# Moving SBUF tiles by 64 to 192 bytes: the start offsets of a PE-bound encoder layer's matmul operands

## The chip, the core and the metric

The kernel runs on one core of a Trainium2 chip. The metric is the device time of one execution in microseconds (us); three runs of the kernel before gave a median of 1275.18 us. One further execution was taken with the hardware profiler; views of its trace are quoted below.

## What is computed

One layer of a bidirectional encoder on 512 tokens of 1024 features, in float32: a half-step SwiGLU feed-forward block, a mixer (a dilated-window attention branch A, a grouped-query attention branch B, gates, an output projection), a second half-step SwiGLU, a final norm.

```python
x = x + 0.5 * swiglu(rmsnorm(x, g1), w1, w3, w2)       # 1024 -> 2816 -> 1024
h = rmsnorm(x, gm)
proj = h @ w_in                                        # A: q, k, v; B: q, k, v; gates
mix = (sigmoid(gA) * (o_a @ P_A) + sigmoid(gB) * (o_b @ P_B)) @ w_out
x = x + mix
x = x + 0.5 * swiglu(rmsnorm(x, g2), w1, w3, w2)
y = rmsnorm(x, g)
```

## The kernel before

**Products in three matmuls.** Every float32 operand is split into a high and a low part (a copy that rounds, then a subtraction), and each product is made of three matmuls on TensorE (PE) in `mm3`: high by high (L233), then the two mixed ones (L234 and L235). Each matmul has a stationary operand of 128 columns, loaded by its own weight load (PEld in the profile), and a moving operand of 256 or 512 columns that is streamed through. In the trace the load for a matmul begins as the matmul ahead of it begins: while one matmul's moving operand is read from SBUF, the stationary operand of the next is read from SBUF too.

**Weights.** All weights come in chunks of 128x1024 by DMA into raw tiles (`wr`, `wa`, `wt`, `ws`), are split by ScalarE (L218) and VectorE (L219) into a pair `wh`, `wl`, and one pair feeds 24 matmuls: 8 slices of 128 columns by three. Below, such a group of 24 is called a tile of work. There are three pairs in the pool `wb` (the main pairs). A fourth pair (tag `whx` in `prep`, L207) lies in whichever pool `self.wx` names, and serves each fourth chunk (`n % 4 == 3`) of the kinds `sw` and `w2`, and of `wb` while branch B's projection runs. In the trace all of them have the name `wh` or `wl`.

**Stages.** Each feed-forward block begins with plain products of 512 columns (`feat`, moving `hH`, `hL`). Then it alternates between stages of a Strassen-like scheme (`strassen`: moving operands of 256 columns from `hH`, `hL`, `TH`, `TL`; outputs `mm`, `X`, `Y`) and the down projection (`blocks`: moving `gg`, 512 columns). The first block has three such rounds, starting with 14, 28 and 21 tiles of 256-column work; the second has 21, 28 and 21. In the last round of the second block half of the down projection is done in 256 columns. The mixer first projects tokens (`token`: there the weights move, 512 columns, and `hH` is stationary), then has one stage of 35 tiles of 256-column work for q and k of branch A (moving `hH`, `TQH`), then 512-column work of many kinds between the attention steps, then `wab` and `wo` (moving `oH`, `qH`, `mH`). In all, 168 tiles of work have 256-column moving operands in these stages: 168 x 24 = 4032 matmuls. 41 of the 168 use the fourth pair.

**Where tiles lie.** Pools are stacked in SBUF from the left in the order in which they are opened, some from the right (`side="right"`: `hH`, `hL`, `TH`, `TL`, `V0`, `V1`). A tile's start byte (the same in each partition) is the sum of all that stands ahead of it. In the pool `tmp` the kernel before reserves a tile `even` of 64 bytes that nothing uses; all that is opened behind it from the left starts 64 bytes later for it. The order of the PE's instructions is written out by the program itself; the other engines' order is set by the recording layer.

Of the kernel before, what the change touches and what calls it, by code (L numbers as in the profile page):

```python
# [11 lines left out]
F32 = mybir.dt.float32  # L12
# [57 lines left out]
class Layer:  # L70
    def __init__(self, ctx, tc, a):
        self.tc, self.nc, self.a = tc, tc.nc, a
        ctx.enter_context(tc.manual_schedule(engines={mybir.EngineType.PE}))
        pool = lambda n, **k: ctx.enter_context(tc.tile_pool(name=n, **k))
        self.dram = pool("dram", bufs=1, space=DRAM)
        self.cst = pool("cst", bufs=1)
        self.wb = pool("wb", bufs=1)
        self.tmp = pool("tmp", bufs=4)
        self.tmp.tile([128, 16], F32, tag="even", name="even", bufs=1)
        self.psm = pool("psm", bufs=4, space=PSUM)  # L80
        self.psa = pool("psa", bufs=4, space=PSUM)
        nc = self.nc
        c = self.cst
        self.x = [c.tile([128, T], F32, name=f"x{d}") for d in range(NK)]
        self.par = c.tile([128, 48], F32, name="par")
        nc.scalar.dma_start(self.par, a["par"])
        self.ident = c.tile([128, 128], F32, name="ident")
        self.ones = c.tile([128, 1], F32, name="ones")
        nc.vector.memset(self.ones, 1.0)
        self.mhalf = c.tile([128, 4], F32, name="mhalf")  # L90
        nc.vector.memset(self.mhalf, -0.5)
        nc.scalar.activation(self.ones, self.ones, AF.Copy)
        self.r = c.tile([128, 8], F32, name="r")
        self.R = c.tile([128, T], F32, name="R")
        nc.gpsimd.memset(self.R, 0.0)
        self.acc = c.tile([128, T], F32, name="acc")
        self.open_h()
        self.gate_d = self.dram.tile([16, 128, T], F32, name="gate_d")
        self.qk_d = self.dram.tile([2 * NSQ, 128, T], F32, name="qk_d")
        self.items = ([("v", 0), ("v", 1), ("sw", 0), ("v", 2)] + [("g", j) for j in range(2)]  # L100
                      + [("qk", f) for f in range(NSQ, 12)] + [("g", j) for j in range(2, 9)]
                      + [("b", g) for g in range(3)] + [("g", j) for j in range(9, 16)])
        span = {"v": ("wav", 4), "qk": ("waq", 2), "g": ("wg", 1), "b": ("wb", 4)}
        self.order = self.ffn_order("a")
        for kind, n in self.items:
            if kind == "sw":
                self.order += [("swq", at) for at in self.slots(range(0, NSQ, 2))]
                continue
            name, m = span[kind]
            self.order += [(name, m * n + i) for i in range(m)]  # L110
        self.order += [("wab", i) for i in range(12)] + [("wo", i) for i in range(8)]
        self.order += self.ffn_order("b")
        self.raws, self.tiles, self.used, self.wx, self.TQ = {}, [], 0, None, None
        self.cap = len(self.order)
        self.rings = {k: [] for k in BUFS}
        self.index = {it[:2]: n for n, it in enumerate(self.order)}
        self.kind = [self.home(it) for it in self.order]
        self.todo = sorted((n for n, t in enumerate(self.kind) if t != "ws"), key=self.turn_of)
# [22 lines left out]
    def open_h(self):  # L141
        self.hctx = ExitStack()
        hp = self.hctx.enter_context(self.tc.tile_pool(name="hp", bufs=1, side="right", reuse_waits="tile"))
        self.hH = [hp.tile([128, T], F32R, name=f"hH{d}") for d in range(NK)]
        self.hL = [hp.tile([128, T], F32R, name=f"hL{d}") for d in range(NK)]

    def split(self, dst_pool, src, shape, tagH, tagL):
        nc = self.nc
# [265 lines left out]
    def ffn(self, s, gin, gnext, hooks, out=None, side=None):  # L414
        with ExitStack() as ctx:
            pool = lambda n, **k: ctx.enter_context(self.tc.tile_pool(name=n, reuse_waits="tile", **k))
            tp = pool("hT", bufs=1, side="right")
            self.TH = tp.tile([128, 3, 4, 256], F32R, name="TH")
            self.TL = tp.tile([128, 3, 4, 256], F32R, name="TL")
            self.wx = pool("wx", bufs=1)  # L420
            self.cp = pool("c", bufs=2)
            self.ffn_run(s, gin, gnext, hooks, out, side or {}, pool("g", bufs=1))
            self.wx = None

# [256 lines left out]
    def project_qk(self):  # L681
        nc, tc = self.nc, self.tc
        with ExitStack() as ctx:
            pool = lambda n, **k: ctx.enter_context(tc.tile_pool(name=n, reuse_waits="tile", **k))
            tp = pool("qT", bufs=1)
            self.TQ = [tp.tile([128, 4, 4, 256], F32R, name=f"TQ{c}") for c in "HL"]
            self.wx = pool("wxq", bufs=1)
            cp, qp = pool("cq", bufs=2), pool("qo", bufs=2)
            steps = self.tq_steps(cp)
            hooks = {7: self.stat_r, 12: self.stat_R, 17: self.stat_p}  # L690
            for n, _ in enumerate(self.stream(self.items[:2])):
                if n in hooks:
                    hooks[n]()
                if n > 8 and n % 4 == 0 and steps:
                    steps.pop(0)()
            assert not steps
            c = {}

            def scaled(dst, src, a, perm, neg):
                src, dst = src.rearrange("p (j n) -> p j n", j=2), dst.rearrange("p (j n) -> p j n", j=2)  # L700
                R = (self.acc if perm else self.R).unsqueeze(1).to_broadcast([128, 2, T])
                if perm:
                    src = src.rearrange("p j (m r) -> p j r m", r=4)
                    dst, R = (t.rearrange("p j (r m) -> p j r m", r=4)[:, :, :, 64 * a:64 * a + 64] for t in (dst, R))
                else:
                    dst, R = (t[:, :, 256 * a:256 * a + 256] for t in (dst, R))
                if neg:
                    for j in range(2) if perm else (slice(0, 2),):
                        nc.vector.scalar_tensor_tensor(dst[:, j], src[:, j], -1.0, R[:, j], op0=ALU.mult, op1=ALU.mult)
                else:  # L710
                    nc.vector.tensor_mul(dst, src, R)

            def store(f, part, t):
                i = 2 * f + part
                nc.gpsimd.dma_start(self.qk_d[i:i + 3:2].rearrange("c p n -> p c n"), t.rearrange("p (c n) -> p c n", c=2))

            def evict(f, step, ps):
                perm = PAIRS[f][1] > 0
                if step == "A11":
                    c[f] = (cp.tile([128, 1024], F32, tag="c1", name="c1"), self.tmp.tile([128, T], F32, tag="t", name="c2"))  # L720
                c1, c2 = c[f][:2]
                lo, hi = c1[:, :T], c1[:, T:]
                if step == "A11":
                    nc.scalar.copy(lo, ps)
                elif step == "S1":
                    nc.scalar.copy(c2, ps)
                elif step == "S2":
                    nc.scalar.copy(hi, ps)
                elif step == "A12":
                    nc.vector.tensor_add(lo, ps, lo)  # L730
                elif step == "S3":
                    nc.vector.tensor_add(c2, ps, c2)
                elif step == "S4":
                    nc.vector.tensor_add(hi, ps, hi)
                    o = qp.tile([128, 1024], F32, tag="qo", name="qo")
                    scaled(o, lo, 0, perm, False)
                    scaled(o, hi, 1, perm, False)
                    store(f, 0, o)
                else:
                    o = qp.tile([128, 1024], F32, tag="qo", name="qo")  # L740
                    scaled(o, ps, 0, perm, True)
                    scaled(o, c2, 1, perm, True)
                    store(f, 1, o)

            for _ in self.strassen("q", range(0, NSQ, 2), evict):
                pass
            self.wx = self.TQ = None
# [478 lines left out]
```

## Time and profile before

| what | value |
|---|---|
| median of three runs | 1275.18 us (1275.02 to 1275.36) |
| profiled execution | 1274.42 us, of which the span of its instructions is 1272.6 us |
| PE busy, matmuls | 1259.8 us, 99% of the span, 8002 matmuls |
| VectorE, ScalarE busy | 888.7 us (70%), 587.2 us (46%) |
| granted PE clock | 0.997 of full speed on average |

How to read it: a matmul's busy time is longer than the distance to the next matmul's start, since matmuls overlap in the pipeline and their ends are modelled. What a matmul costs is the distance between starts: a row of the timeline begins with the start in us from the beginning of the span, then the modelled duration in us.

### The profile page before, as it was taken

What the parts mean: (1) busy time and instruction counts of PE and PEld (TensorE: products, weight loads), DVE (VectorE), ACT (ScalarE), POOL (GpSimd) and SP (SyncE); (2) the same over time, 40 slices, a digit from 0 to 9 for tenths busy, and PEclk for the clock granted to TensorE, in tenths of its full rate; (3) what the DMA queues carried; (4) which work ended last, traced back from release to release, by engine and by line L of the source; (5) the groups of instructions that cost most, each with busy time, mean ns of one, the idle gap of its engine ahead of it and who ended that gap; (6) DMA issues with size and microseconds to landing.
All of it is one profiled execution on the core that took longest, in us unless ns stands there. A gap on an engine that the chain in (4) does not pass through costs nothing.

```text
span 1272.6 us, 19956 instructions
## 1 busy us (share of the span) xinstructions
PE 1259.8 (99%) x8002; PEld 1119.1 (88%) x8002; DVE 888.7 (70%) x1339; ACT 587.2 (46%) x867; POOL 118.7 (9%) x124
## 2 busy tenths in 40 slices
PE   9999999999999999999999999999999999999997
PEld 7897999899889999877878878888889989988996
DVE  8784688468784885766557898655677747875775
ACT  8551355145463443644234466543475415532553
POOL 1111110000210212100001100000301001100001
PEclk9999999999999999999999999999999999999998
DMA  9875766342484936533232310446737536744222
GB/s 301 229 186 164 189 195 184 99 100 67 135 229 133 237 118 244 167 102 99 84 104 83 116 50 25 128 160 190 217 99 180 169 100 183 185 147 115 55 80 67
DMA packets 85549, 181.91 MB, mean 143 GB/s; under 512 B 12480, under 2 KB 19024, under 8 KB 85456
## 3 DMA queue, kind: packets, MB, share of 16 engines
q1 hardware_dynamic: 67904, 140.74, 33.2%
q0 software_dynamic: 16832, 39.34, 15.3%
q8 instruction: 63, 1.03, 0.3%
q10 hardware_dynamic: 720, 0.55, 0.1%
q14 instruction: 30, 0.25, 0.1%
HBM read 168.98 MB, written 15.29 MB: 145 GB/s over the span
## 4 chain that ended last, share of the span: by engine, by line
PE 91%; DVE 4%; issue 1%; DMA 1%; ACT 1%; POOL 0%; SPq 0%; POOLq 0%; DVEq 0%
PE mm L233 24%; PE mm L235 23%; PE mm L234 23%; PE Y L233 4%; PE Y L235 3%; PE Y L234 3%; PE X L233 2%; PE X L235 2%; PE X L234 2%; PE mm L837 1%; PE Tb L976 1%; PE S L786 1%; PE T L855 1%; DMA d<-SO 1%; DVE wl L219 1%
## 5 line engine op out<-in xcount | busy, mean ns | idle before, releaser
L218 ACT CAST wh<-wr 128x1024 fp32r<-128x1024 f32 x142 | 148.9, 1049 | 216.1 <-PE mm L234 142.2
L219 DVE TENSOR_TENSOR wl<-wr,wh 128x1024 fp32r<-128x1024 f32 x142 | 173.7, 1224 | 55.2 <-ACT wh L218 54.8
L233 PE MATMUL mm<-hH,wh 128*128 128x256 f32 (+1 forms) x600 | 200.7, 335 | 0.0
L235 PE MATMUL mm<-hH,wl 128*128 128x256 f32 (+1 forms) x600 | 196.7, 328 | 0.9 <-DVE wl L219 0.9
L234 PE MATMUL mm<-hL,wh 128*128 128x256 f32 (+1 forms) x600 | 196.3, 327 | 0.2 <-DVE hL L370 0.2
L233 PE MATMUL mm<-gg,wh 128*128 128x512 f32 (+1 forms) x376 | 142.2, 378 | 0.0
L234 PE MATMUL mm<-gg,wh 128*128 128x512 f32 (+1 forms) x376 | 142.0, 378 | 0.0
L235 PE MATMUL mm<-gg,wl 128*128 128x512 f32 (+1 forms) x376 | 141.3, 376 | 0.0
L233 PEld LDWEIGHTS mm<-hH,wh 128*128 128x128 f32 x600 | 113.2, 189 | 14.2 <-issue 3.2
L235 PEld LDWEIGHTS mm<-hH,wl 128*128 128x128 f32 x600 | 113.0, 188 | 12.2 <-DVE wl L219 1.3
L234 PEld LDWEIGHTS mm<-hL,wh 128*128 128x128 f32 x600 | 113.2, 189 | 10.4 <-DVE hL L370 0.8
L218 ACT CAST wh<-wa 128x1024 fp32r<-128x1024 f32 x48 | 50.4, 1050 | 101.7 <-PE mm L234 47.3
L501 DVE TENSOR_TENSOR u<-mm,R 128x512 f32<-128x512 f32 (+1 forms) x52 | 33.8, 650 | 82.4 <-PE mm L235 82.1
L219 DVE TENSOR_TENSOR wl<-wt,wh 128x1024 fp32r<-128x1024 f32 x48 | 58.8, 1224 | 37.7 <-ACT wh L218 37.0
L235 PE MATMUL mm<-TH,wl 128*128 128x256 f32 x304 | 84.3, 277 | 0.0
L234 PE MATMUL mm<-TL,wh 128*128 128x256 f32 x304 | 84.3, 277 | 0.0
L233 PE MATMUL mm<-TH,wh 128*128 128x256 f32 x304 | 84.3, 277 | 0.0
L233 PEld LDWEIGHTS mm<-gg,wh 128*128 128x128 f32 x376 | 70.6, 188 | 14.9 <-PE mm L235 0.9
L218 ACT CAST wh<-ws 128x1024 fp32r<-128x1024 f32 x48 | 50.5, 1051 | 70.1 <-PE mm L234 51.6
L235 PEld LDWEIGHTS mm<-gg,wl 128*128 128x128 f32 x376 | 70.6, 188 | 13.4
L234 PEld LDWEIGHTS mm<-gg,wh 128*128 128x128 f32 x376 | 70.7, 188 | 12.6
L219 DVE TENSOR_TENSOR wl<-wa,wh 128x1024 fp32r<-128x1024 f32 x48 | 58.6, 1221 | 31.0 <-ACT wh L218 30.9
(233 smaller groups left out, 3172.5 us busy)
## 6 DMA issues: line engine op xcount, KB each, us to landing
wr<-in_w2a SPq DMA_DIRECT2D x22, 512.0 KB, 3.3
wr<-in_w2b SPq DMA_DIRECT2D x22, 512.0 KB, 3.3
wt<-in_w13b SPq DMA_DIRECT2D x20, 512.0 KB, 4.3
wa<-in_w13b SPq DMA_DIRECT2D x20, 512.0 KB, 3.4
wt<-in_w13b POOLq DMA_DIRECT2D x20, 512.0 KB, 5.9
wt<-in_w13a SPq DMA_DIRECT2D x18, 512.0 KB, 3.4
wt<-in_w13a POOLq DMA_DIRECT2D x18, 512.0 KB, 6.1
wa<-in_w13a SPq DMA_DIRECT2D x18, 512.0 KB, 3.5
```

The costliest lines, as they stand in the source:

```text
L218: self.nc.scalar.copy(H, raw)
L219: self.nc.vector.tensor_sub(L, raw, f32(H))
L233: mm(out, lH, rH, start=start, stop=False, skip_group_check=more)
L234: mm(out, lH, rL, start=False, stop=False, skip_group_check=more)
L235: mm(out, lL, rH, start=False, stop=stop, skip_group_check=more)
L501: nc.vector.tensor_mul(u, ps, R)
L786: nc.tensor.matmul(*args, start=True, stop=True)
L837: nc.tensor.matmul(oc, v, p, start=st, stop=sp)
L855: nc.tensor.transpose(ps[:, 128 * b:128 * b + 128], P[h][:, c0 + 128 * b:c0 + 128 * b + 128], self.ident)
L976: nc.tensor.transpose(pt[:, 128 * j:128 * j + 128], P[h, j][:, 128 * k:128 * k + 128], self.ident)
```

## The change

The tile `even` is removed. A helper `shifted` reserves a filler tile of n bytes at the head of a pool, and four pools get one: `wx` and `c` in the feed-forward blocks (128 bytes each), `qT` and `wxq` in the projection of q and k (64 bytes each).

```diff
         self.tmp = pool("tmp", bufs=4)
-        self.tmp.tile([128, 16], F32, tag="even", name="even", bufs=1)
...
+    @staticmethod
+    def shifted(pool, n):
+        pool.tile([128, n // 4], F32, tag="shift", name="shift", bufs=1)
+        return pool
...
-            self.wx = pool("wx", bufs=1)
-            self.cp = pool("c", bufs=2)
+            self.wx = self.shifted(pool("wx", bufs=1), 128)
+            self.cp = self.shifted(pool("c", bufs=2), 128)
...
-            tp = pool("qT", bufs=1)
+            tp = self.shifted(pool("qT", bufs=1), 64)
             self.TQ = [tp.tile([128, 4, 4, 256], F32R, name=f"TQ{c}") for c in "HL"]
-            self.wx = pool("wxq", bufs=1)
+            self.wx = self.shifted(pool("wxq", bufs=1), 64)
```

No instruction is added, removed or moved on any engine; the lists of what an instruction waits for differ in nine DMA issues and one VectorE instruction, since a shifted tile covers other old tiles than before. What changes is where tiles start. Summed up from the pools, the start bytes are, modulo 256 (all tiles of a kind are equal there; slices of 128 or 256 columns begin 512 or 1024 bytes further on, which leaves them equal):

| tiles | before | after |
|---|---|---|
| main pairs `wh`, `wl` (first at byte 50080) | 160 | 160 |
| `hH`, `hL`, `TH`, `TL`, `TQH`, `TQL`, `V0`, `V1` (hH0 at 196576) | 224 | 224 |
| fourth pair in the feed-forward blocks and in the q, k stage (first block: byte 120288, then 120352) | 224 | 32 |
| fourth pair in branch B's projection | 224 | 160 |
| `gg` (first at 136672, then 136864) | 224 | 160 |
| `oH`, `oL`, `qH`, `qL`, `mH`, `mL`, `kH`, `vH`, `PTH`, `Pb`, `P`, `qk`, `V2` | 224 | 160 |

Call distance the start of the moving operand less the start of the stationary operand that is loaded meanwhile, modulo 256. It changes like this:

| work | matmuls | distance before | after |
|---|---|---|---|
| 256 columns, main pairs | 3048 | 64 | 64 |
| 256 columns, fourth pair | 984 | 0 | 192 |
| `gg`, 512 columns, main pairs | 720 | 64 | 0 |
| `gg`, 512 columns, fourth pair | 264 | 0 | 128 |
| `wab` and `wo`, 512 columns | 480 | 64 | 0 |
| `gg`, 256 columns (end of the kernel), main / fourth | 96 / 48 | 64 / 0 | 0 / 128 |
| plain products with moving `hH`, 512 columns | 768 | 64 | 64 |
| tokens, moving main pairs | 504 | 192 (180 to 192 in the dilated groups) | the same |
| tokens of branch B, moving fourth pair | 72 | 0 | 192 |

## The prediction

> **What bounds the kernel now.** I read the page first, then the busy times of one stage, then the waits, then the timeline tile by tile.
>
> ```profile
> span 1272.6 us, 19956 instructions
> PE 1259.8 (99%) x8002; PEld 1119.1 (88%) x8002; DVE 888.7 (70%) x1339; ACT 587.2 (46%) x867; POOL 118.7 (9%) x124
> ...
> PE 91%; DVE 4%; issue 1%; DMA 1%; ACT 1%; POOL 0%; SPq 0%; POOLq 0%; DVEq 0%
> ```
> ```profile
> 140.00:217.00 77.00, 77.00 (x666) 76.80 (x666) 62.22 (x63) 41.75 (x47) 8.33 (x7) 1.00 0.72 190
> ```
> ```profile
> PE warm L1102 <- POOL R L95: 1.3, 1, 1.3
> ```
>
> PE is busy 99% of the span and makes 91% of the chain. In the 256-column stage from 140 to 217 us it is busy all the time, VectorE 62.22 of 77.00 us (81%), the DMA engines 0.72; the clock is 1.00. The longest wait of PE on anybody is 1.3 us. So the time is the sum of the distances between matmul starts, and the question is what sets such a distance. The timeline answers. These rows are the first matmuls of five tiles of work in a row, 24 matmuls each, at the head of a 256-column stage; the second tile uses the fourth pair.
>
> ```profile
> 138.41 0.28 PE L233 MATMUL mm<-hH,wh 128*128 128x256 f32 x1
> ...
> 141.23 0.28 PE L233 MATMUL Y<-TH,wh 128*128 128x256 f32 x1
> ...
> 144.10 0.28 PE L233 MATMUL mm<-TH,wh 128*128 128x256 f32 x1
> ...
> 146.82 0.28 PE L233 MATMUL X<-hH,wh 128*128 128x256 f32 x1
> ...
> 149.54 0.28 PE L233 MATMUL mm<-hH,wh 128*128 128x256 f32 x1
> ```
>
> The first tile takes 2.82 us, 117.5 ns per matmul. The second, whose distance (moving less stationary start, modulo 256) is 0, takes 2.87 us, 119.6 ns. The third and fourth, at distance 64 like the first, take 2.72 us, 113.3 ns. Going through the heads of all 168 tiles like this, the 41 on the fourth pair run at 119.9 ns on average (2.88 us), whichever of `hH`, `TH`, `TQH` they read; the 127 on the main pairs run at 113.3 ns (107 tiles) or 117.8 (20 tiles: one or two at the head of a stage, six in the first stage of each feed-forward block). These are the first and the last of the 20, each with the head of the next tile:
>
> ```profile
> 52.90 0.28 PE L233 MATMUL mm<-hH,wh 128*128 128x256 f32 x1
> ...
> 55.73 0.28 PE L233 MATMUL Y<-TH,wh 128*128 128x256 f32 x1
> ...
> 1172.03 0.28 PE L233 MATMUL Y<-TH,wh 128*128 128x256 f32 x1
> ...
> 1174.86 0.28 PE L233 MATMUL mm<-TH,wh 128*128 128x256 f32 x1
> ```
>
> So the distance sets the pace, and at distance 64 there are two paces, of which a tile keeps the one that it comes in with.
>
> ```profile
> 953.94 0.28 PE L233 MATMUL X<-hH,wh 128*128 128x256 f32 x1
> ...
> 956.82 0.28 PE L233 MATMUL mm<-hH,wh 128*128 128x256 f32 x1
> ...
> 959.65 0.28 PE L233 MATMUL mm<-hH,wh 128*128 128x256 f32 x1
> ...
> 965.30 0.28 PE L233 MATMUL Y<-hH,wh 128*128 128x256 f32 x1
> ...
> 968.17 0.28 PE L233 MATMUL mm<-TH,wh 128*128 128x256 f32 x1
> ...
> 970.89 0.28 PE L233 MATMUL mm<-TH,wh 128*128 128x256 f32 x1
> ```
>
> Here the tiles from 953.94 and 965.30 us are on the fourth pair. The first takes 2.88 us and the next tile is still slow (2.83 us); the second takes 2.87 us and from there on it is 2.72. Every change from 117.8 to 113.3 in the trace happens across such a tile at distance 0.
>
> At 512 columns it is the other way round. The third interval below is `gg` on the fourth pair (distance 0), the two ahead of it are `gg` on the main pairs (64); then the head of the second tile of `wab` and that of `wo`, 264 matmuls apart (64); then tokens, 48 matmuls apart (192); then a plain product behind tokens, 18 matmuls apart (64).
>
> ```profile
> 232.23 0.39 PE L233 MATMUL mm<-gg,wh 128*128 128x512 f32 x1
> ...
> 237.72 0.39 PE L233 MATMUL mm<-gg,wh 128*128 128x512 f32 x1
> ...
> 243.22 0.39 PE L233 MATMUL mm<-gg,wh 128*128 128x512 f32 x1
> ...
> 248.65 0.39 PE L233 MATMUL mm<-gg,wh 128*128 128x512 f32 x1
> ...
> 817.74 0.39 PE L233 MATMUL mm<-qH,wh 128*128 128x512 f32 x1
> ...
> 878.17 0.39 PE L233 MATMUL mm<-mH,wh 128*128 128x512 f32 x1
> ```
> ```profile
> 642.41 0.39 PE L233 MATMUL mm<-wh,hH 128*128 128x512 f32 x1
> ...
> 653.61 0.40 PE L233 MATMUL mm<-wh,hH 128*128 128x512 f32 x1
> ...
> 712.04 0.40 PE L233 MATMUL mm<-hH,wh 128*128 128x512 f32 x1
> ...
> 716.24 0.40 PE L233 MATMUL mm<-hH,wh 128*128 128x512 f32 x1
> ```
>
> Per matmul that is 229 ns at distance 64, 226.3 (over all such rows 226.7) at distance 0, 233.3 at 192, and 233.3 at 64 for as long as the pace of the tokens is kept.
>
> **The change part by part.** No instruction moves; each part is a count of matmuls times a change of pace, all of it on PE's path.
>
> ```profile
> L233 PE MATMUL mm<-gg,wh 128*128 128x512 f32 x328 | 128.5, 392 | 0.0
> ...
> L233 PE MATMUL mm<-qH,wh 128*128 128x512 f32 x64 | 25.2, 394 | 0.0
> L233 PE MATMUL mm<-mH,wh 128*128 128x512 f32 x64 | 25.2, 394 | 0.0
> ...
> L233 PE MATMUL mm<-gg,wh 128*128 128x256 f32 x48 | 13.6, 284 | 0.0
> L233 PE MATMUL mm<-oH,wh 128*128 128x512 f32 x32 | 12.6, 394 | 0.0
> ```
>
> Each row is one of three lines, so `gg` has 984 matmuls of 512 columns (720 on main pairs) and 144 of 256, and `wab` with `wo` has 480.
>
> - 256 columns on the fourth pair: 984 matmuls leave distance 0 for 192. The trace has no 256-column matmul at 192. Nearest rows: 113.3 ns at distance 64, which is as far from 0 on the other side, and 119.9, the price now. No 256-column row is cheaper than 113.3, so that is the lower end, and I take it: 984 x (113.3 - 119.9) = -6.5 us. The upper end is worse than now: tokens show 192 as the dearest at 512 columns, 6.6 ns above distance 0; that on top gives +6.5 us.
> - 256 columns on the main pairs keep distance 64, but what lies ahead of them changes. The later stages (all but the first of each feed-forward block and the one for q and k) now begin behind `gg` at distance 0 or 128 instead of 64. Some of the 20 slow tiles may go: 0 to -20 x 24 x 4.5 ns = -2.2 us. Twelve look likely to go (six at the heads of later stages, six that follow a switch that failed, as at 953.94 us); I take half of them: -0.6 us, which leaves 14 slow tiles.
> - `gg`, 512 columns, main pairs: 720 x (226.7 - 229) = -1.6 us.
> - `wab` and `wo`: 480 x (226.7 - 229) = -1.1 us.
> - `gg`, 512 columns, fourth pair: 264 matmuls from 0 to 128, which the trace does not show. Between 226.7 and 233.3, so 0 to +1.7 us (no 512-column row is cheaper than 226.7, so a gain is left out); I take 0, for want of a row that speaks for more.
> - Small ones: `gg` in 256 columns at the end goes from 64 to 0 for 96 matmuls, +0.2 us; tokens of branch B on the fourth pair from 0 to 192, 72 x 6.6 ns = +0.5 us at most, half taken, since those groups are six matmuls long and end before a pace has set in. The transposes of the attentions (from 96 to 160) are not shown at their new distance either:
>
> ```profile
> L976 PE MATMUL Tb<-ident,Pb 128*128 128x128 f32 x128 | 19.4, 272 | 0.2 <-DVE Pb L970 0.2
> ...
> L855 PE MATMUL T<-ident,P 128*128 128x128 f32 x120 | 15.7, 272 | 0.0
> ```
>
> 248 times the spread of 6.6 ns of the 256-column rows is 1.6 us either way; I take 0.
> - VectorE reads moved tiles. In these two rows one input starts at 160 and at 224 modulo 256, the other at 160 in both:
>
> ```profile
> L219 DVE TENSOR_TENSOR wl<-wr,wh 128x1024 fp32r<-128x1024 f32 x142 | 173.7, 1224 | 55.2 <-ACT wh L218 54.8
> L219 DVE TENSOR_TENSOR wl<-wt,wh 128x1024 fp32r<-128x1024 f32 x48 | 58.8, 1224 | 37.7 <-ACT wh L218 37.0
> ```
>
> Both take 1224 ns, so nothing is put down there, nor for ScalarE, which has slack (41.75 of 77.00 us). The changed wait lists concern tiles that were let go stages earlier: nothing. A PE that is 1% faster brings VectorE from 81 to 82% of a 256-column stage, so nothing new becomes the bound.
>
> Sum: -6.5 - 0.6 - 1.6 - 1.1 + 0.2 + 0.3 = -9.3 us. The profiled execution took 1274.4 us, 0.8 below the median of the three runs; on the median it is 1275.2 - 9.3 = 1265.9, said as 1266.
>
> **A rule against it.** The Trainium skill, page "SBUF — State Buffer", section "Who interferes with whom", gives PE two independent read ports, one for the moving operand and one for the weight load, and says that PE never waits on anyone. By that rule start bytes could not matter, and the sum would be 0 us. The trace disagrees: 119.6 against 113.3 ns between neighbouring tiles that differ in the start byte alone. [...]
>
> **The rivals.**
>
> Slow pace kept (slower). A tile at distance 0 is what ends the 117.8 pace. If distance 192 does not, and itself runs at that pace, the stages keep what they come in with. A tile at 117.8 instead of 113.3 costs 24 x 4.5 ns = 0.11 us. If all 168 stay slow: 4032 x 117.8 = 475.0 us. Now it is 107 x 24 x 113.3 + 20 x 24 x 117.8 + 984 x 119.9 = 465.5, so +9.5; with the -2.2 of the other parts +7.3 us, 1282.5. It decides once some 100 of the 168 tiles are slow (the 14 of my sum and 86 more, 86 x 0.11 = 9.3). For it: 712.04 us, where a plain product keeps the pace of distance 192. Against: half of the work is entered from 512 columns at distance 0, and behind 256 columns at distance 0 the trace nearly always has 113.3.
>
> Slow pace in first stages only. The stages entered from plain products or tokens have 14 + 35 + 21 = 70 tiles. If they all stay slow and the others are fast, that is 56 more slow tiles than in my sum: +6.0, in all -3.3 us, 1271.9.
>
> Distance 192 stays dear at 256 columns. At 119.9 the first term is gone: -2.8 us, 1272.4. At 126.5 it is +3.7, 1278.9. For it: tokens at 233.3.
>
> The page's rule, no change: 1275.2.
>
> **How the numbers follow.** Chances: my forecast, with smaller shares of slow tiles, 0.48; slow pace throughout 0.13; in first stages only 0.15; distance 192 dear 0.20; no change 0.04. 0.2% is 2.6 us, about what a measurement of this kernel can tell from no change. Faster by over that: 0.48, and about half each of the first-stage case and of the dear distance, which lie at the edge (-3.3, -2.8): 0.66. Within: 0.15. Slower: 0.13 and the dear end of the fourth, 0.19. The range: 1263 is the forecast with all 20 slow tiles gone and transposes a little cheaper; 1278 leaves out the slow pace throughout and the worst of distance 192. The likeliest case's own range is 1263 to 1270.
>
> **What would show it.** Right: fourth-pair tiles of 2.72 us, and `wab` rows 226.7 ns apart. Wrong in the first term: fourth-pair tiles of 2.87 us or more. Wrong by the slow pace: main-pair tiles of 2.82 us through whole stages. The forecast as a whole is wrong if the 256-column stages together do not lose about 7 us.

## The result, and the profile after

The changed kernel takes 1268.9 us (median of five, 1268.5 to 1269.3), the kernel before beside it 1275.2 us (five, 1274.9 to 1275.8). The ratio is 0.995, 95% interval 0.9939 to 0.9962: faster by 6.3 us, or 0.5%. The forecast was 1266.0 with 1263 to 1278, so direction and range hold, and the gain is two thirds of the 9.3 us that it summed up. In a later comparison on one chip (below) it was 1269.5 us, ratio 0.9953 (0.994 to 0.9967).

The profiled execution took 1268.5 us. From the page of the kernel after, the span, the busy times and the chain's shares:

```profile
span 1266.7 us, 19954 instructions
...
PE 1254.0 (99%) x8002; PEld 1113.0 (88%) x8002; DVE 888.2 (70%) x1339; ACT 587.3 (46%) x867; POOL 118.6 (9%) x124
...
PE 93%; DVE 3%; issue 1%; DMA 1%; ACT 1%; POOL 0%; SPq 0%; POOLq 0%; DVEq 0%
```

The span is 5.9 us shorter, PE's busy time 5.8 us; VectorE and ScalarE are where they were. The same 77 us window of a 256-column stage as before (start and end, length, then busy time and count of PE, PEld, VectorE, ScalarE and GpSimd, the granted clock, DMA share and rate):

```profile
140.00:217.00 77.00, 77.00 (x672) 76.66 (x671) 63.30 (x64) 42.19 (x48) 8.33 (x7) 1.00 0.73 189
```

PE is without a gap in both, at the same clock, and starts 672 matmuls where it started 666. So the time came out of the times from start to start. These are heads of tiles of work in the kernel after, in the timeline: five at the head of a later stage (the second on the fourth pair), two at the head of the first stage, `gg` with the fourth pair in the third interval, two rows of `wab` and `wo` with 264 matmuls between them, and four around the first two fourth-pair tiles of the second block's first stage.

```profile
53.54 0.28 PE L237 MATMUL mm<-hH,wh 128*128 128x256 f32 x1
...
56.37 0.28 PE L237 MATMUL Y<-TH,wh 128*128 128x256 f32 x1
...
138.69 0.28 PE L237 MATMUL mm<-hH,wh 128*128 128x256 f32 x1
...
141.52 0.28 PE L237 MATMUL Y<-TH,wh 128*128 128x256 f32 x1
...
144.24 0.28 PE L237 MATMUL mm<-TH,wh 128*128 128x256 f32 x1
...
146.96 0.28 PE L237 MATMUL X<-hH,wh 128*128 128x256 f32 x1
...
149.68 0.28 PE L237 MATMUL mm<-hH,wh 128*128 128x256 f32 x1
...
231.47 0.39 PE L237 MATMUL mm<-gg,wh 128*128 128x512 f32 x1
...
236.91 0.39 PE L237 MATMUL mm<-gg,wh 128*128 128x512 f32 x1
...
242.36 0.40 PE L237 MATMUL mm<-gg,wh 128*128 128x512 f32 x1
...
247.95 0.39 PE L237 MATMUL mm<-gg,wh 128*128 128x512 f32 x1
...
820.27 0.39 PE L237 MATMUL mm<-qH,wh 128*128 128x512 f32 x1
...
880.11 0.39 PE L237 MATMUL mm<-mH,wh 128*128 128x512 f32 x1
...
950.03 0.28 PE L237 MATMUL X<-hH,wh 128*128 128x256 f32 x1
...
952.86 0.28 PE L237 MATMUL mm<-hH,wh 128*128 128x256 f32 x1
...
961.34 0.28 PE L237 MATMUL Y<-hH,wh 128*128 128x256 f32 x1
...
964.06 0.28 PE L237 MATMUL mm<-TH,wh 128*128 128x256 f32 x1
```

Divide the intervals by 24. In the later stage the first tile is still slow (2.83 us, 117.9 ns); the tile on the fourth pair, 2.87 us before, now takes 2.72 (113.3 ns), and so do those behind it. `gg` on the main pairs went from 229 to 226.7 ns (5.44 us a tile), on the fourth pair from 226.3 the other way, to 232.9 (5.59 us). `wab` and `wo` are at 59.84 us / 264 = 226.7. The first stage still begins at 117.9, and as before the first tile on the fourth pair there does not end that pace (950.03: 2.83 us, and the next tile as well), while the second does (961.34: 2.72 us).

All starts of the two traces, summed by kind of work (time from each matmul's start to the next; the changes are taken before rounding):

| work | matmuls | before, us (mean ns) | after, us (mean ns) | change |
|---|---|---|---|---|
| 256 columns, fourth pair | 984 | 118.0 (119.9) | 111.8 (113.6) | -6.2 |
| 256 columns, main pairs | 3048 | 347.6 (20 of 127 tiles at 117.8) | 347.6 (the same 20) | 0.0 |
| `gg`, 512, main | 720 | 165.1 (229.4) | 163.9 (227.7) | -1.2 |
| `gg`, 512, fourth | 264 | 60.3 (228.4) | 61.8 (234.0) | +1.5 |
| `wab`, `wo` | 480 | 109.9 (228.9) | 108.8 (226.7) | -1.1 |
| `gg`, 256 columns | 144 | 18.0 | 18.1 | +0.2 |
| tokens of branch B, fourth | 72 | 16.8 (232.7) | 17.0 (235.5) | +0.2 |
| everything PE starts | 8002 | 1264.4 | 1258.3 | -6.1 |

### The profile page after: what moved, and what is told of

Same layout as the page of the kernel before. It is cut to its first block, busy times and chain, and to the rows that moved or that the text cites. A ratio compares the mean times of both kernels' runs of the same rounds, so it can differ in the third digit from the quotient of the medians.

```text
span 1266.7 us, 19954 instructions
## 1 busy us (share of the span) xinstructions
PE 1254.0 (99%) x8002; PEld 1113.0 (88%) x8002; DVE 888.2 (70%) x1339; ACT 587.3 (46%) x867; POOL 118.6 (9%) x124
## 4 chain that ended last, share of the span: by engine, by line
PE 93%; DVE 3%; issue 1%; DMA 1%; ACT 1%; POOL 0%; SPq 0%; POOLq 0%; DVEq 0%
PE mm L237 24%; PE mm L239 24%; PE mm L238 23%; PE Y L237 3%; PE Y L239 3%; PE Y L238 3%; PE X L239 2%; PE X L237 2%; PE X L238 2%; PE S L790 1%; PE mm L841 1%; PE Tb L980 1%; PE T L859 1%; DVE wl L223 0%; PE Sb L237 0%
```

## The experiments

Below, distance always means that of the start bytes (modulo 256). The theory, of which the forecast used one half: the distance sets a matmul's pace, and at distance 64 a slow pace that a stage comes in with stays until the distance changes (theory A). The rivals: the fourth pair was slow for another reason than its distance (it is another buffer, higher in memory), or an even distance of 64 would be as good as the mixture.

**A map of distances.** A kernel of matmuls alone, in one chain, with the layer's pattern of high and low operands, the moving operand at each distance, in blocks of 48; ahead of the first block stand 24 matmuls of 512 columns at 64, ahead of the second 48 of 256 columns at 0. This kernel and the two later ones of matmuls alone ran once each.

```diff
+        def block(n, d, tiles):
+            m = slice(512 + d // 4, 512 + d // 4 + n)
+            for i in range(8 * tiles):
+                s = slice(128 * (i % 8), 128 * (i % 8) + 128)
+                for w, v in ((wh, mh), (wh, ml), (wl, mh)):
+                    mm(bank[:, :n], w[:, s], v[:, m], start=first[0], stop=False, skip_group_check=True)
...
+                block(512, 64, 1)
+                block(n, d, 2)
+                block(256, 0, 2)
+                block(n, d, 2)
```

> A kernel of matmuls alone, with no part of the layer: the same triple (high by high, two mixed), one pair of weights, the moving operand started at 16 distances from 0 to 240 bytes (and at 320 and 448) from the stationary one, in 256 and in 512 columns, each behind a 512-column block at distance 64 and once more behind a 256-column block at distance 0. Theory (the distance modulo 256 sets the pace): 256 columns 120 ns at 0, 113.3 or 117.8 at 64 and at 192; 512 columns 226.7 at 0, 229 at 64, 233.3 at 192, 234 at 128; 320 and 448 as 64 and 192. Rival (what sets the pace is something else that goes with the fourth pair, such as its place above byte 100000 or who wrote it): no dependence on the distance.

Heads of its blocks in the timeline, for distance 64 and for 112; each time the first block, the 48 at distance 0, the second block, and the next distance's 512-column work. The last two rows are the first block of 512 columns at distance 128 and the work behind it:

```profile
105.62 0.28 PE L43 MATMUL bank<-mh,wh 128*128 128x256 f32 x1
...
111.06 0.28 PE L43 MATMUL bank<-mh,wh 128*128 128x256 f32 x1
...
116.81 0.28 PE L43 MATMUL bank<-mh,wh 128*128 128x256 f32 x1
...
122.47 0.40 PE L43 MATMUL bank<-mh,wh 128*128 128x512 f32 x1
...
173.49 0.28 PE L43 MATMUL bank<-mh,wh 128*128 128x256 f32 x1
...
178.95 0.28 PE L43 MATMUL bank<-mh,wh 128*128 128x256 f32 x1
...
184.70 0.28 PE L43 MATMUL bank<-mh,wh 128*128 128x256 f32 x1
...
190.20 0.40 PE L43 MATMUL bank<-mh,wh 128*128 128x512 f32 x1
...
689.20 0.39 PE L43 MATMUL bank<-mh,wh 128*128 128x512 f32 x1
...
700.35 0.28 PE L43 MATMUL bank<-mh,wh 128*128 128x256 f32 x1
```

At 64 the first block takes 5.44 us (113.3 ns each), the second, same operands, 5.66 (117.9): two paces, by what ran ahead. At 112 it is 5.46 and 5.50 us, so 113.7 and 114.6 with the change of pace in them, and 113.3 in the later half of both. The 48 of 512 columns at 128 take 11.15 us, 232.3 ns each. Of all the distances (later half of each block, ns, first / second block):

| distance | 256 columns | 512 columns |
|---|---|---|
| 0 | 120.0 / 120.0 | 226.7 / 226.7 |
| 64 | 113.3 / 117.8 | 228.9 / 233.3 |
| 112 | 113.3 / 113.3 | 231.1 / 231.1 |
| 128 | 118.8 / 118.6 | 232.7 / 232.3 |
| 192 | 117.8 / 113.3 | 233.3 / 233.3 |
| the eleven others | 116.7 to 120.0 | 230.0 to 236.7 |
| 320 and 448 | as 64 and 192 | 233.3 |

The distance sets the pace, together with what ran ahead: 64 has two paces at either width, and 192 has two at 256 columns. The two distances above 256 fit the ones that are 256 less (at 512 columns 320 shows only the dearer pace of 64). 0 is the best distance for 512 columns, and at 256 columns only 112 shows 113.3 behind both kinds of work. For `gg` on the fourth pair the map has what the trace of before lacked: 128 costs 232.3 to 232.7 ns. The rival that the fourth pair's place or history makes it slow gives no such dependence: here one pair of weights shows all these paces.

**Without a change of distance.** The fourth pair at the main pairs' byte offset (160), so that the 168 tiles are all at 64 and all `gg` at 0. The lines are shown against the kernel before; the helper `shifted` is added as in the change.

```diff
-        self.tmp.tile([128, 16], F32, tag="even", name="even", bufs=1)
...
-            tp = pool("qT", bufs=1)
+            tp = self.shifted(pool("qT", bufs=1), 64)
...
-            self.wx = pool("wxq", bufs=1)
+            self.wx = self.shifted(pool("wxq", bufs=1), 192)
```

> The fourth pair at 160 modulo 256 like the main pairs: distance 64 for all 256-column work, 0 for all of gg. Theory A (only a change of distance ends the slow pace): gg on the fourth pair gains 264 x (227 - 234) = -1.8 us against the changed kernel, but every 256-column stage keeps the pace of its head, 117.8: up to 148 more slow tiles x 0.108 = +16 us; near 1283 us. Rival B (the slow pace ends by itself after some tiles): about 1267 us.

Measured: 1282.8 us, ratio to before 1.0058 (1.0043 to 1.0073). The stage that begins at 138.69 in the kernel after, here:

```profile
138.76 0.28 PE L237 MATMUL mm<-hH,wh 128*128 128x256 f32 x1
...
141.59 0.28 PE L237 MATMUL Y<-TH,wh 128*128 128x256 f32 x1
...
144.41 0.28 PE L237 MATMUL mm<-TH,wh 128*128 128x256 f32 x1
...
147.24 0.28 PE L237 MATMUL X<-hH,wh 128*128 128x256 f32 x1
```

2.83, 2.82, 2.83 us: every one of the 168 tiles runs at 117.8 ns. The pair's own place is no cause, and the odd pair of the kernel before did pay for something: its 119.9 ns brought the 113.3 of the others. This is the forecast's rival "slow pace kept", to within 0.3 us of its 1282.5; it needed the fillers left out.

**Each half alone.** First the fourth pair at 32 as in the kernel after, with `gg` and the mixer's tiles left at 224; then the other way round. Both are shown against the kernel after.

```diff
+        self.tmp.tile([128, 16], F32, tag="even", name="even", bufs=1)
...
-            self.wx = self.shifted(pool("wx", bufs=1), 128)
-            self.cp = self.shifted(pool("c", bufs=2), 128)
+            self.wx = self.shifted(pool("wx", bufs=1), 64)
+            self.cp = self.shifted(pool("c", bufs=2), 192)
...
-            tp = self.shifted(pool("qT", bufs=1), 64)
+            tp = pool("qT", bufs=1)
```

> Only the fourth pair is moved for the 256-column work (distance 0 to 192); gg, oH, qH, mH stay at 224 as in the kernel before. Theory: -6.2 us from the fourth pair at 113.3, gg on the fourth pair goes from distance 0 to 192, 264 x (233.3 - 227) = +1.7: -4.5 us against the kernel before, 1270.7. Rival (the gain came from the 512-column side): no change, 1275.

Measured: 1271.3 us, 0.9965 (0.9951 to 0.9979). Fourth-pair tiles 113.6 ns as in the kernel after; 14 slow tiles instead of 20; `gg` on the main pairs 231.0 instead of 229.4, on the fourth pair (now 192) 234.2. `gg` on the main pairs is dearer because ten of its tiles, behind a fourth-pair tile at 192, keep a pace of 233.3 ns, the dearer one of the map at 64. The stage that was slow at its head in the kernels before and after begins here at the fast pace, 2.72 us a tile:

```profile
139.00 0.28 PE L238 MATMUL mm<-hH,wh 128*128 128x256 f32 x1
...
141.72 0.28 PE L238 MATMUL Y<-TH,wh 128*128 128x256 f32 x1
...
144.44 0.28 PE L238 MATMUL mm<-TH,wh 128*128 128x256 f32 x1
```

```diff
-            self.wx = self.shifted(pool("wx", bufs=1), 128)
-            self.cp = self.shifted(pool("c", bufs=2), 128)
+            self.wx = self.shifted(pool("wx", bufs=1), 64)
+            self.cp = self.shifted(pool("c", bufs=2), 192)
...
-            self.wx = self.shifted(pool("wxq", bufs=1), 64)
+            self.wx = pool("wxq", bufs=1)
```

> Only the 512-column operands gg, oH, qH, mH are moved to 160; the fourth pair stays at distance 0 from the 256-column operands. Theory: gg on the main pairs -1.2 and wab, wo -1.1 us, gg on the fourth pair to distance 192 +1.7, small ones +0.5: about 0, 1275. Rival (the 512-column side carries the gain): 1270 or less.

Measured: 1275.3 us, 1.000 (0.9991 to 1.001). The gain on `gg`'s main pairs, `wab` and `wo` is 2.2 us by its trace, and 1.6 of it go back on `gg` with the fourth pair (234.3 ns at 192). So alone the 256-column half gains 4.2 us (against the 1275.55 of the kernel before beside it) and the 512-column half nothing, while the two together gain 6.3. They don't add up, mainly because `gg` on the fourth pair is at 192 in either half and pays some 1.5 us there, and pays that once in the whole change, at 128. And the 256-column half alone got rid of six of the slow tiles, which are there again in the whole change, where the later stages are entered from `gg` at 0. In the kernel before, though, these stages are entered from `gg` at 64 as well, and begin slow; there the fourth pair's `gg`, one or two tiles ahead of that, is at 0, and in the 256-column half alone it is at 192. So 64 right ahead is not enough for a fast start.

**What ends the slow pace, first try.** Matmuls alone again. The distance was changed by moving the moving operand.

```diff
+        for d in DISTANCES:
+            block(512, 0, 8)
+            block(256, 64, 16)
+            block(256, d, 8)
+            block(256, 64, 16)
```

> A kernel of matmuls alone, it computes none of the layer. First series, for each distance X in steps of 16 bytes: 24 matmuls of 512 columns at distance 0, 48 of 256 columns at 64, 24 at X, 48 at 64. The 48 ahead of X should run at 118 ns, as they do behind the last stage of gg in the layer. Theory A (any change of distance ends the slow pace): behind every X but 64 the last 48 run at 113.3 ns. Theory B (only some distances end it, by what they leave in the way the operands are read): behind 0 and 192 113.3, behind some of the others 118. Second series: the same behind 24 matmuls of 512 columns at 64, where 256 columns at 64 start at 113.3 ns; A says nothing of whether X takes this pace away, B expects that some X do. Third series: X = 0 and 192 for 3, 12, 48 and 96 matmuls in the first series' place; A: 113.3 ns behind all eight. Fourth: 48 matmuls at 104, 108, 116 and 120, for how wide the place at 112 is: 113.3 ns if it is 16 bytes wide, 118 to 120 if it is 112 alone.

From its timeline the rows for X = 192: the 24 at 192, the 48 at 64 behind them, the next block.

```profile
255.74 0.28 PE L43 MATMUL bank<-mh,wh 128*128 128x256 f32 x1
...
258.56 0.28 PE L43 MATMUL bank<-mh,wh 128*128 128x256 f32 x1
...
264.22 0.40 PE L43 MATMUL bank<-mh,wh 128*128 128x512 f32 x1
```

2.82 us for 24 (117.5 ns), then 5.66 us for 48 (117.9): neither does 192 run at 113.3 here, nor does it end the slow pace. Nor does 0, for 3, 12, 24, 48 or 96 matmuls; only X = 16 and 48 do. Entered from 512 columns at distance 0, all 16 sequences began slow; from 512 columns at 64, ten of 16 began at 113.3. Where they began at 113.3, X = 80, 160, 176 and 224 took that pace away, and 16, 32, 48, 64, 144 and 208 kept it. The fourth series found 112 to be narrow: 104, 108, 116 and 120 run at 120.0 to 130.0 ns in the later halves of their blocks. So theory A as written there (any change of distance) is dead. B is right that only some distances end or bring the slow pace, but 0 and 192, which it expected to end it, do not.

**Second try.** The same with the stationary operand moved instead, as in the layer.

```diff
+        for w in range(0, 256, 16):
+            block(512, 0, 0, 8)
+            block(256, 64, 0, 16)
+            block(256, 64, w, 8)
+            block(256, 64, 0, 16)
```

> Matmuls alone again, none of the layer. In the map of resets, moving operands at other distances for 24 matmuls did not end the slow pace behind 512-column work at distance 0, at 0 and 192 neither, though the fourth pair of the layer ends it at both. What is left of the difference: in the layer the stationary operand moves and the moving one stays, the addresses are others, and the results go to changing banks and halves of a bank. First series: 48 matmuls of 256 columns at distance 64 behind 24 of 512 at 0, 24 with the stationary operand moved up by O (0 to 240 in steps of 16), 48 at 64. Theory C (the pace hangs on a change of the stationary operand's byte offset): behind O = 64 and 128, the fourth pair's before and after, the last 48 run at 113.3 ns. Second series: O = 128 with both operands moved on by 0 to 224 bytes: if absolute offsets count, the pace behind differs among the eight. Third series: results to changing banks and halves, with O = 128, O = 64, and the moving operand at 0 and 192, behind 24, 48, 72 and 96 matmuls. Theory D (banks or halves): 118 behind all O of the first series, 113.3 in the third. If neither shows 113.3 behind O = 64 and 128, what ends the slow pace in the layer stays open.

Rows for O = 128 and O = 192: the 24 with the stationary operand moved, the 48 behind them, the next block.

```profile
177.29 0.28 PE L50 MATMUL bank<-mh,wh 128*128 128x256 f32 x1
...
180.02 0.28 PE L50 MATMUL bank<-mh,wh 128*128 128x256 f32 x1
...
185.46 0.39 PE L50 MATMUL bank<-mh,wh 128*128 128x512 f32 x1
...
255.23 0.29 PE L50 MATMUL bank<-mh,wh 128*128 128x256 f32 x1
...
258.08 0.28 PE L50 MATMUL bank<-mh,wh 128*128 128x256 f32 x1
...
263.74 0.40 PE L50 MATMUL bank<-mh,wh 128*128 128x512 f32 x1
```

Behind O = 128 the 48 take 5.44 us (113.3 ns), and the 24 themselves 2.73; behind O = 192 it is 5.66 (117.9). Of the 16 offsets only 64 (itself 119.7 ns), 128 (113.4) and 144 (118.6) end the slow pace. 64 and 128 are the fourth pair of the kernel before and of the kernel after, with the layer's own numbers. Second series: O = 128 ends it at all eight places (steps of 32 bytes), so there the absolute start bytes don't count. Third: with changing banks, O = 64 and 128 end it, the moving operand at 0 and 192 does not. Theory D falls. C's forecast for 64 and 128 holds; but 12 of the 15 moves of the stationary operand end nothing, so a move as such is not what does it.

**`w2` off the fourth pair.** In the kernel after, so that all of `gg`'s 512-column work is at distance 0.

```diff
-        tag = "whx" if self.order[n][0][:2] in ("sw", "w2", "wb") and n % 4 == 3 and self.wx is not None else "wh"
+        tag = "whx" if self.order[n][0][:2] in ("sw", "wb") and n % 4 == 3 and self.wx is not None else "wh"
```

> The kernel after, with the w2 tiles taken off the fourth weight pair: all 984 matmuls of 512 columns from gg are then at distance 0. If distance 128 is what costs 234.0 ns there, the 264 of them go to 227.7: 264 x 6.3 ns = 1.7 us less than 1268.9, so 1267.2 us, with 1266.8 to 1267.8. Rival: the other pair's 234 ns has nothing to do with the distance (the pair lies higher in memory, or its weights come later): then no gain, or, with one pair fewer to prepare w2 ahead in, waits and 1269 to 1275 us. The 256-column work keeps its 20 slow tiles.

Measured: 1268.4 us (1268.2 to 1268.5), 0.9942 (0.9925 to 0.9958). In its timeline the tile of `gg` that took 5.59 us:

```profile
241.39 0.39 PE L237 MATMUL mm<-gg,wh 128*128 128x512 f32 x1
...
246.83 0.39 PE L237 MATMUL mm<-gg,wh 128*128 128x512 f32 x1
```

5.44 us, 226.7 ns; all of `gg`'s 512-column work is 1.8 us shorter, as expected. But the time was above the 1267.8 allowed. The trace has the transposes of branch A's weights (`T`) 1.4 us longer and the tokens on the main pairs 0.8 us longer. So both kernels once more, side by side, five rounds:

> The same kernel again (w2 off the fourth pair), beside the kernel after on one chip. In its first profile gg gained the 1.8 us, but the transposes of branch A's weights took 1.4 us more and the token tiles 0.8 us more than in the kernel after, and the time was only 0.5 us below it. Theory: that loss goes with the execution, not with the edit; then the transposes take other values this time in both kernels (14.4 to 15.8 us were seen in seven profiles), and the difference of the medians lies between 0.5 and 2 us. Rival: the edit brings it (the order of the weight loads in the layer before is another): then 15.8 us here and 14.4 in the kernel after again, and the medians 0.3 to 0.7 us apart.

> The changed kernel again, for the comparison on one chip: 1268.5 to 1269.3 us; the transposes of branch A's weights at 14.4 us if the program sets them, anywhere from 14.4 to 15.8 if the execution does.

Measured: 1268.1 us (1267.7 to 1269.1) against 1269.5 (1268.8 to 1269.9), 1.4 us apart. The transposes took 15.4 us in both, so that loss went with the execution. The kernel after was 0.2 us above the range expected of it. The tokens on the main pairs again took 121.5 us against 120.7: those 0.8 us belong to the edit. They lie in the mixer's first token tile. PE waits there, at 353 us, for VectorE's `acc`, in both runs of the edit and in neither of the kernel after:

```profile
PE stat L398 <- DVE acc L384: 0.6, 1, 0.6
```

Why VectorE is later there was not tried.

**The map used.** All four weight pairs at 160 and the moving operands of the 168 tiles at 16, distance 112, with `gg` at 0 throughout. The 16 bytes come from slices that begin four elements into larger tiles.

```diff
-        self.hH = [hp.tile([128, T], F32R, name=f"hH{d}") for d in range(NK)]
-        self.hL = [hp.tile([128, T], F32R, name=f"hL{d}") for d in range(NK)]
+        self.hH, self.hL = ([t[:, 4 + T * d:4 + T * d + T] for d in range(NK)]
+                            for t in (hp.tile([128, NK * T + 64], F32R, name=n) for n in ("hH0", "hL0")))
+        self.shifted(hp, HP)
...
-            self.TH = tp.tile([128, 3, 4, 256], F32R, name="TH")
-            self.TL = tp.tile([128, 3, 4, 256], F32R, name="TL")
-            self.wx = self.shifted(pool("wx", bufs=1), 128)
-            self.cp = self.shifted(pool("c", bufs=2), 128)
+            self.TH, self.TL = (tp.tile([128, 3136], F32R, name=f"T{c}")[:, 4:3076].rearrange("p (c k n) -> p c k n", c=3, k=4) for c in "HL")
+            self.wx = pool("wx", bufs=1)
+            self.cp = pool("c", bufs=2)
```

(HP is 224 bytes; `TQH` and `TQL` are sliced likewise, with fillers of 96 and 160 bytes in `qT` and `wxq`.)

> All 256-column operands at distance 112 from all four pairs (the fourth pair at the others' byte offset, so that gg is at 0 from all four; h at 112 also for the 512-column work on it). If the distance alone sets the pace, and 112 has the one fast pace that the map of distances showed, then none of the 168 tiles runs at 118: against the kernel after 22 x 24 x 4.5 ns = 2.4 us less, gg on the fourth pair 1.7 us less, h with 512 columns 0 to 1.7 us more (231.1 ns against 228.9 in the map), the first tiles behind gg about 0.3 us more: 1265.1 to 1266.8 us. Rival, a pace that only a change of distance ends, whatever the distance: with no change left all 168 tiles run at 118, 146 x 24 x 4.6 ns = 16 us more, and the time is 1281 to 1284 us as in the run without fillers.

Measured: 1266.0 us (1265.6 to 1266.6), 0.9924 (0.9909 to 0.9939) to before, below both kernels. The head of the later stage, and `gg` on the fourth pair:

```profile
137.97 0.28 PE L239 MATMUL mm<-hH,wh 128*128 128x256 f32 x1
...
140.73 0.28 PE L239 MATMUL Y<-TH,wh 128*128 128x256 f32 x1
...
143.45 0.28 PE L239 MATMUL mm<-TH,wh 128*128 128x256 f32 x1
...
241.40 0.39 PE L239 MATMUL mm<-gg,wh 128*128 128x512 f32 x1
...
246.84 0.39 PE L239 MATMUL mm<-gg,wh 128*128 128x512 f32 x1
```

The first tile behind `gg` takes 2.76 us (115.0 ns), all others 2.72: seven tiles at 115.1 ns, one a stage, and 161 at 113.3. `gg` on the fourth pair is at 226.7. The rival of this run, a pace that only a change ends, would have given 1281 and more: at 112 no slow pace stays. Against the kernel after the 168 tiles take 2.1 us less and `gg` in 512 columns 1.8 us less; part of that is lost elsewhere in this trace, 1.0 us of it in the transposes `T`, which vary by as much between runs of one kernel.

## Why the prediction came out as it did

**That PE's times from start to start are the whole time:** right. They account for 6.1 us of the two traces, whose spans are 5.9 us apart, with the busy times of the other engines unchanged.

**256 columns on the fourth pair, -6.5:** measured -6.2. The value taken, 113.3, is what 39 of the 41 tiles run at; two, the first in each feed-forward block, keep 118. The reason given for it (192 lies as far from 0 as 64 does) was weak: with the moving operand moved to 192, the same distance ran at 117.5 ns behind slow work, and in the map it has both paces. With the stationary operand moved, as in the layer, it was 113.4 there. So the size was right partly by luck: at 117.8 the term would have been -2.1. Nor did the forecast's rows tell the start byte from the pair itself, as its neighbouring tiles differ in both; the run without fillers did, where the same pair has the pace of the others.

**`gg`, 512 columns, fourth pair, 0 with a bound of +1.7:** the step that failed, by the largest sum. "I take 0, for want of a row that speaks for more" measured +1.5; taking `w2` off that pair gave 1.8 back, and the map has 128 near the dear end. The forecast had rows for three distances at 512 columns, 226.7, 229 and 233.3, with 0 the cheapest; in hindsight, a distance that none of them shows was more likely to be like the other two.

**Slow tiles, -0.6:** measured 0; all 20 stay, at the same places. Half of the idea was right: with `gg` left at 64 (the first half alone) six do go. But `gg` at 0 is the other half of the change, and behind 512 columns at 0 the 256-column work at 64 began slow all 16 times in the second experiment with matmuls alone. The change's two halves work against each other there, which the sum treated as one. With this the 256-column stages lost 6.2 us where the forecast had 7.1, and the two terms, 1.5 and 0.6, are about two thirds of the 3.0 us by which the gain fell short.

**"Every change from 117.8 to 113.3 in the trace happens across such a tile at distance 0":** true of the trace, wrong as a cause. The same distance reached from the moving side ends nothing; a stationary operand moved by 64 or 128 does, with matmuls alone. The forecast's case survived since the change moves the stationary side, from the one of these to the other.

**`gg`, main pairs, -1.6:** measured -1.2. The price was read off single tiles (229 and 226.7); the means over all 720 are 229.4 and 227.7. In both kernels six `bps` matmuls (L600 before) stand among those of the first round and make their neighbours dearer, and in the kernel after the first tile behind a stage or behind the fourth pair is at 227.1 to 228.2. **`wab` and `wo`, -1.1:** measured -1.1. **The small ones:** +0.2 for `gg` in 256 columns, as put down, and +0.2 for branch B's tokens, put down as +0.3. The transposes of branch A (`T`), 0.4 us shorter here, lay between 14.4 and 15.8 us in nine profiles of the layer, with two values for one and the same kernel, so nothing can be read from them at this size. What was not in the sum: `PTH` and `kH` as moving operands, +0.2 each, and the plain products with `hH`, +0.4, which spread by as much between profiles of one kernel (185.0 and 184.4).

**The rivals:** "distance 192 stays dear" fell at the fourth-pair tiles of 2.72 us; "slow pace kept" and "first stages only" at the main tiles behind them. The price of "slow pace kept" was right, though, as the run without a change of distance showed. The no-change rule, from the Trainium skill's page "SBUF — State Buffer", section "Who interferes with whom", does not hold here: matmuls alone, with no other engine at work, were 113.3 to 120.0 ns apart in the map, by start bytes and by what ran ahead.

What stays open: what inside the chip makes the distance count; why two paces exist at 64, and what decides which one a stage begins with; why of the stationary operand's moves only those by 64, 128 and 144 bytes end the slow pace; and why in the first stages, which are entered from plain products at 64, the first tile on the fourth pair fails to end the slow pace and the second succeeds.

## What to carry to other kernels

Where PE is busy without gaps, read the time from start to start of the same matmul at several places of the timeline: if it differs at full clock, the operands' start bytes are a cause worth trying, and a filler tile of some bytes is a cheap trial. Measure the candidates first with matmuls alone, and move the same operand as the kernel would, with the same work ahead, since the pace depends on both. Choose a distance that is good from every entry rather than one that is good behind a certain tile.

## What the runs showed of the hardware

- With float32r operands in this high and low pattern the spacing of matmuls depends on the start of the moving operand less that of the stationary operand loaded meanwhile, modulo 256 bytes, and on what ran ahead: 113.3 to 130.0 ns at 256 columns, 226.7 to 236.7 at 512, at a granted clock of 0.996 to 0.998.
- At 64 there are two lasting paces, 113.3 and 117.8 ns. With matmuls alone, moving the stationary operand for 24 matmuls by 64, 128 or 144 bytes ends the slow one and by the other multiples of 16 it does not; 128 does so at all eight absolute places tried. In the layer the first such tile of each feed-forward block does not end it.
- The best distance for 512 columns, 0, is among the dearest for 256 (120.0), and puts the 256-column work at 64 behind it into its slow pace. 112 has 113.3 alone once it has set in (115.1 in a stage's first tile), and 4 bytes to either side cost 120.0 ns or more.
